# Gate weights for all 128 first keys in one pass over the tokens, beside the second half of the expert activations

## The chip, the cores and the metric

One core of a Trainium2 chip runs the program. The metric is the device time of one execution in microseconds.

## The reference, cut to what matters

Two transformer blocks run one after the other on 256 tokens of width 1024. The change touches the feed-forward part of the first, a layer of 16384 experts with one vector each for input and output. For each token and each of 8 heads it scores 128 first and 128 second keys, takes the best 16 pairs, and sums 16 experts:

```python
cand_i = (top_i[..., 0, :, None] * PEER_KEYS + top_i[..., 1, None, :]).reshape(b, s, PEER_HEADS, PEER_TOPK * PEER_TOPK)
best_v, best_pos = lax.top_k(cand_v, PEER_TOPK)
idx = jnp.take_along_axis(cand_i, best_pos, axis=-1)
gate = jax.nn.softmax(best_v, axis=-1)
...
u = u_tab[ix]
act = jax.nn.gelu(jnp.einsum('chkd,cd->chk', u, hx).astype(jnp.float32))
vv = v_tab[ix]
return jnp.einsum('chk,chkd->cd', (gx * act).astype(vv.dtype), vv)
```

## The kernel before

The kernel doesn't gather experts. It computes all 16384 activations for all tokens, builds a dense matrix of gate weights (zero for experts that a token did not choose), multiplies the two and multiplies the product with the whole value table. An expert is a pair of a first and a second key. A tile holds one first key: 128 second keys on the partitions, tokens along the free dimension. `act[0]` holds first keys 0 to 63, `act[1]` 64 to 127, each 64 x 256 fp32 per partition.

Weights come as fp32 items of 128 x 1024, loaded by SP (`Stream._load`, line 186). ScalarE rounds an item to a high half (line 200), VectorE subtracts to get the low half (line 211), and every product is three fp32r matmuls (line 366): high x high, high x low, low x high. Three pairs of halves exist at a time. When TensorE's next item is taken, `ahead` first issues the low halves still owed, then loads and high halves; with `st.lag` set, as here, an item's low half is issued one item after its high half. So when item j is taken, the low half of item j + 1 goes to VectorE's queue, behind all that the program wrote for VectorE before. Each engine works through its own instructions in the order in which they are written.

The stages around the change:

- `u_phase(0)` computes activations of keys 0 to 63, beside the rest of the routing (`rt`). `u_phase(1)` does keys 64 to 127. A pair of keys is 48 matmuls of 256 columns into one PSUM bank `pa`, and one GELU on ScalarE (line 1253) into `act`.
- `g_phase(half)` builds the gate weights of 64 first keys and multiplies them into `act[half]`. A block is 8 tokens. `prep` makes one-hots in fp16: of the second key (`a`, line 1281), of the first key (`b`, line 1279), and `b` times the gate's high and low part (`c`, line 1283). The 128 partitions of these are the 8 x 16 chosen experts of a token. For each token two matmuls, `a` as weights and the two parts of `c` as moving data, give 128 second keys x 64 first keys (line 1295). VectorE scales that and multiplies it into `act` (line 1297). In `a`, `b` and `c` the 8 tokens are innermost, so the columns of one token lie 8 elements (16 bytes) apart.
- `v_phase(0)` and `v_phase(1)` multiply `act[0]` and `act[1]` with the value table: 12 matmuls of 512 columns for each first key, into four banks `pb` that are summed over both. `need` splits `act` into high and low parts ahead of that.

`weave(main, (side, n))` writes n steps of the side generator after each step of the main one. `g_phase(0)` is woven into `u_phase(1)` at 1.05 steps for each of 64 steps, `g_phase(1)` into `v_phase(0)` at 1.04; each has 64 steps. The one-hot buffers lie in `xt` (the residual, saved to DRAM as `x1d` and loaded back on POOL's queue, line 1348) and in `misc`.

Of the kernel before, what the change touches and what calls it, by code (L numbers as in the profile page):

```python
# [7 lines left out]
F32 = mybir.dt.float32  # L8
FR = mybir.dt.float32r
BF = mybir.dt.bfloat16  # L10
HF = mybir.dt.float16
I32 = mybir.dt.int32
U32 = mybir.dt.uint32
AF = mybir.ActivationFunctionType
OP = mybir.AluOpType
AX = mybir.AxisListType
PSUM = bass.MemoryType.PSUM
# [250 lines left out]
def weave(main, *sides):  # L268

    sides = [[s[0], s[1], s[2] if len(s) > 2 else 0, 0.0] for s in sides]  # L270
    for n, _ in enumerate(main):
        for s in sides:
            if n < s[2]:
                continue
            s[3] += s[1]
            while s[3] >= 1.0 and s[0] is not None:
                s[3] -= 1.0
                if next(s[0], "end") == "end":
                    s[0] = None
# [21 lines left out]
def run(g):  # L301
    for _ in g:
        pass
# [13 lines left out]
def program(ctx, tc, A, out, dbg=None, stop=None, force=False):  # L317
    nc = tc.nc
    V, T, G, E = nc.vector, nc.scalar, nc.gpsimd, nc.tensor

    def dump(name, ap):
        if dbg is not None and name in dbg:
            nc.gpsimd.dma_start(dbg[name], ap)
# [5 lines left out]
    def pool(stack, name, bufs=1, side=None):  # L329
        kw = {} if side is None else {"side": side}  # L330
        return stack.enter_context(tc.tile_pool(name=name, bufs=bufs, reuse_waits="tile", **kw))

    const = pool(ctx, "const")
    strm = pool(ctx, "strm")
    psum = ctx.enter_context(tc.tile_pool(name="psum", bufs=4, space=PSUM))
    resid = pool(ctx, "resid")
    small = pool(ctx, "small", 3)
    x1d = ctx.enter_context(tc.tile_pool(name="dram", bufs=1, space=bass.MemoryType.DRAM)).tile([128, 2, D], F32, name="x1d")
# [11 lines left out]
    def pa():  # L350
        return psum.tile([128, 512], F32, name="pa")

    def pb():
        return psum.tile([128, 512], F32, name="pb")

    def load_const(p, name, eng=None):
        t = p.tile(list(A["c_" + name].shape), F32, name="c_" + name)
        (eng or nc.gpsimd).dma_start(t, A["c_" + name])
        return t
# [5 lines left out]
    def mm(p, a, b, s, e):  # L365
        E.matmul(p, a, b, start=s, stop=e)  # L366
# [23 lines left out]
    def flat(ap):  # L390
        return ap.rearrange("p a b -> p (a b)")
# [84 lines left out]
    xt = resid.tile([128, 2, D], F32, name="xt")  # L476
# [12 lines left out]
    misc = pool(phr, "pmisc", side="right").tile([128, 2048], F32, name="misc")  # L489
# [333 lines left out]
    for m in range(NF):  # L823
        st.add("ffn", A["w_ffn"], 3 * m, 3 * m + 2)
        if m >= LAG:
            q = m - LAG
# [30 lines left out]
    with Pools() as pha:  # L857
# [43 lines left out]
        iota = load_const(const, "iota")  # L901
# [161 lines left out]
        for h in range(6):  # L1063
            heads.append(dict(q=qk[:, h], k=qk[:, 6 + h // 3], v=(lambda kt, h=h: va[:, kt, (h // 3) * 128:(h // 3) * 128 + 128]),
                              base=0, d=128, first=True, last=True, i=h, finish=fin(0), mode="win",
                              scale=128.0 ** -0.5, mask=wmask, sinkb=sinkb))
# [62 lines left out]
    act = [None, pool(ph1, "pR", side="right").tile([128, 64, 256], F32, name="act1")]  # L1129
# [4 lines left out]
    keys = act[1][:, 16:24].rearrange("p a (b c) -> p (a b) c", b=2)  # L1134
# [41 lines left out]
    def routing():  # L1176
        V.tensor_copy(io16, iota[:, :16, None].to_broadcast([128, 16, 16]))
        for tt in range(2):
# [63 lines left out]
    weave(lin_fm("pq", range(0, 16, 2), XH, XL, lambda m, p: T.activation(flat(qf[:, m:m + 2]), p, AF.Copy)),  # L1242
          (rt, 2.7, 8))

    def u_phase(half):
        blk = Blocks("u")
        for k in range(0, 64, 2):
            p = pa()
            for i in range(2):
                fm_tile(p[:, i * 256:i * 256 + 256], blk, 8, XH, XL)  # L1250
                if i == 0:
                    yield
            T.activation(flat(act[half][:, k:k + 2]), p, AF.Gelu_apprx_tanh)  # L1253
            yield

    weave(u_phase(0), (rt, 2.7))
# [1 line left out]
    dump("idT", idT)  # L1258


    io8 = misc[:, 768:1280].bitcast(HF).rearrange("p (a b) -> p a b", b=8)
    ib = misc[:, 1280:1536].bitcast(HF).rearrange("p (a b) -> p a b", a=2)
    gp = misc[:, 1536:1792].bitcast(HF).rearrange("p (a b) -> p a b", a=2)
    V.tensor_copy(io8, iota[:, :, None].to_broadcast([128, 128, 8]))
    V.tensor_copy(ib, idT[:, 0:2])
    V.tensor_scalar(idT[:, 2], idT[:, 2], 32768.0, None, op0=OP.mult)
    V.tensor_copy(gp[:, 0], idT[:, 2])
    V.tensor_sub(gp[:, 1], idT[:, 2], gp[:, 0])

    oha = [xt[:, 0, i * 512:i * 512 + 512].bitcast(HF).rearrange("p (k t) -> p k t", t=8) for i in range(2)]  # L1270
    ohc = [ap.bitcast(HF).rearrange("p (q k t) -> p q k t", q=2, t=8) for ap in (xt[:, 1, 0:512], misc[:, 0:512])]
    ohb = [xt[:, 1, i:i + 256].bitcast(HF).rearrange("p (k t) -> p k t", t=8) for i in (512, 768)]

    def g_phase(half):

        def prep(n):
            t = slice(n * 8, n * 8 + 8)
            a, b, c = oha[n % 2], ohb[n % 2], ohc[n % 2]
            V.tensor_tensor(b, io8[:, half * 64:half * 64 + 64], ib[:, 0, None, t].to_broadcast([128, 64, 8]),
                            op=OP.is_equal)  # L1280
            V.tensor_tensor(a, io8, ib[:, 1, None, t].to_broadcast([128, 128, 8]), op=OP.is_equal)
            for i in range(2):
                V.tensor_tensor(c[:, i], b, gp[:, i, None, t].to_broadcast([128, 64, 8]), op=OP.mult)

        prep(0)
        yield
        for n in range(32):
            if n < 31:
                prep(n + 1)
                yield  # L1290
            a, c = oha[n % 2], ohc[n % 2]
            p = pa()
            for i in range(8):
                for q in range(2):
                    mm(p[:, i * 64:i * 64 + 64], a[:, :, i], c[:, q, :, i], q == 0, q == 1)
            v = act[half][:, :, n * 8:n * 8 + 8]
            V.scalar_tensor_tensor(v, p.rearrange("p (t k) -> p k t", t=8), 2.0 ** -15, v, op0=OP.mult, op1=OP.mult)  # L1297
            yield

    vacc = []  # L1300
# [13 lines left out]
    def v_phase(half, R, after):  # L1314
        need = v_parts(half)

        def part(X):
            def f(k):
                need(k // 2)
                return X[:, k % 8]  # L1320
            return f
        if half == 0:
            vacc.extend([[pb(), pb()] for _ in range(2)])
        for k in range(64 - R):
            need(k // 2)
            h, l = st.take("vt")
            for t in range(2):
                v_mm(half, k, t, h, l)
            yield
        if R:  # L1330
            held = [st.keep("vt") for _ in range(R)]
            for k in range(64 - R, 64):
                need(k // 2)
            yield from halves(held, lambda t, n, i, h, l: v_mm(half, 64 - R + i, t, h, l, (n,)), after)
# [4 lines left out]
            mm_tm(vacc[t][n], h[:, HS[n]], l[:, HS[n]], YH[:, k % 8, ts], YL[:, k % 8, ts],  # L1339
                  half == 0 and k == 0, half == 1 and k == 63)  # L1340

    g0, g1 = g_phase(0), g_phase(1)
    weave(u_phase(1), (g0, 1.05))
    run(g0)
    dump("act0", act[0])
    weave(v_phase(0, 0, None), (g1, 1.04))
    run(g1)
    nc.gpsimd.dma_start(xt, x1d)
    ph0.close()

    st.extend(pool(ctx, "strmc"), 2, 1, len(st.items), "c")
# [55 lines left out]
    pg = pool(phx, "pg", side="right")  # L1407
# [40 lines left out]
    with Pools() as ph:  # L1448
# [40 lines left out]
        for h in range(12):  # L1489
            b = (h % 2) * 64  # L1490
            heads.append(dict(q=qs[b:b + 64, h // 2], k=kap(h // 4, b),
                              v=(lambda kt, h=h: vs[:, kt, (h // 4) * 64:(h // 4) * 64 + 64]), base=b, d=64,
# [17 lines left out]
    with Pools() as ph:  # L1510
# [10 lines left out]
        for m in range(NF):  # L1521
            p = pa()
# [20 lines left out]
    with Pools() as ph:  # L1543
# [70 lines left out]
        for h in range(12):  # L1614
            b = (h % 2) * 64
            heads.append(dict(q=qf[b:b + 64, h // 2], k=qf[b:b + 64, 6 + h // 2],
                              v=(lambda kt, h=h: vf[:, kt, h * 64:h * 64 + 64]), base=b, d=64,
# [121 lines left out]
    with Pools() as ph:  # L1739
# [186 lines left out]
        for n in range(NE * 11):  # L1926
            e, j = divmod(n, 11)
# [23 lines left out]
        e, yp = NE - 1, yps.pop(NE - 1)  # L1951
        gBe, bBe = st.spare(), st.spare()
        ln_load(3, gBe, bBe)
        a = turn(last)
# [6 lines left out]
        b = [small.tile([128, 2, 6], F32, name="bn") for _ in range(2)]  # L1961
# [34 lines left out]
```

## Time and profile before

| | us |
|---|---|
| median of 3 runs | 2499.32 |
| lowest run | 2498.3 |
| profiled execution | 2496.38 |
| its span, first to last instruction | 2494.6 |

The profile is one execution, taken by the hardware profiler. Engines are PE (TensorE's matmuls), PEld (its weight loads, which overlap matmuls), DVE (VectorE), ACT (ScalarE), POOL and SP. Times are microseconds unless marked ns; `out<-in` are the program's tile names, L366 is line 366. The ends of matmuls are modelled, so the step from one start to the next tells more than the length. Idle time of an engine that isn't the bound costs nothing.

### The profile page before, as it was taken

How to read it: one execution, taken by the hardware profiler on the slowest of the kernel's cores; microseconds unless marked ns; L12 is line 12 of the kernel's file. 1: busy time of each engine (PE TensorE's matmuls, PEld its weight loads, DVE VectorE, ACT ScalarE, POOL GpSimd, SP SyncE). 2: the span in 40 equal slices, each digit the busy share in tenths (PEclk: the TensorE clock that was granted, in tenths of full speed). 3: DMA queues.
4: the chain of work that ended last, by engine and by line, in shares of the span. 5: the costliest groups of instructions: out<-in, count | busy, mean ns of one | idle time of the engine just before them, and what ended most of it. 6: DMA issues, size and time to landing. Idle time of an engine off the chain costs nothing. (4 is left out here: it accounts for less than half of the span.)

```text
span 2494.6 us, 38669 instructions
## 1 busy us (share of the span) xinstructions
PE 2439.9 (98%) x14776; PEld 2125.6 (85%) x14776; DVE 1880.2 (75%) x2923; ACT 1393.0 (56%) x1859; POOL 35.2 (1%) x48
## 2 busy tenths in 40 slices
PE   9999999999999999999999999989899999999997
PEld 8888999999999888788868998768788888888885
DVE  7776669886666666665677548579889999999997
ACT  5775444443333333454544444438677877877775
POOL 0100000000000000000000000000000000000000
PEclk9999999999999999999999999989999999999999
DMA  7345555554444444756524554359899999999992
GB/s 266 117 132 181 186 178 180 175 173 133 143 136 141 139 135 143 254 187 190 174 93 178 186 195 146 121 217 336 307 340 346 368 341 344 366 355 338 363 357 89
DMA packets 149652, 545.62 MB, mean 219 GB/s; under 512 B 16960, under 2 KB 17088, under 8 KB 148816
## 3 DMA queue, kind: packets, MB, share of 16 engines
q1 hardware_dynamic: 145728, 528.55, 61.5%
q0 software_dynamic: 2720, 10.50, 1.3%
q10 hardware_dynamic: 1008, 4.00, 0.4%
q8 instruction: 118, 1.93, 0.3%
q14 instruction: 78, 0.64, 0.1%
HBM read 540.88 MB, written 2.10 MB: 218 GB/s over the span
## 5 line engine op out<-in xcount | busy, mean ns | idle before, releaser
L200 ACT ACTIVATE hwb<-rawb 128x1024 fp32r<-128x1024 f32 (+1 forms) x406 | 428.5, 1057 | 333.6 <-PE pa L366 132.5
L211 DVE TENSOR_TENSOR lwb<-rawb,hwb 128x1024 fp32r<-128x1024 f32 (+1 forms) x406 | 493.5, 1224 | 77.0 <-ACT hwb L200 75.1
L366 PE MATMUL pa<-XH,hwb 128*128 128x256 f32 x1848 | 509.1, 283 | 0.4 <-ACT XH L502 0.3
L366 PE MATMUL pa<-XH,lwb 128*128 128x256 f32 x1848 | 501.8, 280 | 2.7 <-DVE lwb L211 2.6
L366 PE MATMUL pa<-XL,hwb 128*128 128x256 f32 x1848 | 500.9, 279 | 0.0
L366 PEld LDWEIGHTS pa<-XH,hwb 128*128 128x128 f32 x1848 | 341.6, 188 | 4.4 <-issue 1.3
L366 PEld LDWEIGHTS pa<-XH,lwb 128*128 128x128 f32 x1848 | 340.2, 188 | 5.1 <-DVE lwb L211 4.9
L366 PEld LDWEIGHTS pa<-XL,hwb 128*128 128x128 f32 x1848 | 340.5, 188 | 1.1
L211 DVE TENSOR_TENSOR lwb<-rawe,hwb 128x1024 fp32r<-128x1024 f32 x176 | 210.9, 1222 | 23.9 <-ACT hwb L200 19.0
L200 ACT ACTIVATE hwb<-rawe 128x1024 fp32r<-128x1024 f32 x176 | 185.7, 1058 | 25.5 <-PE pb L366 11.6
L211 DVE TENSOR_TENSOR lwb<-rawf,hwb 128x1024 fp32r<-128x1024 f32 x130 | 156.6, 1222 | 17.8 <-ACT hwb L200 13.0
L1297 DVE SCALAR_TENSOR_TENSOR act<-pa,act 128x512 f32<-128x512 f32 x64 | 44.3, 692 | 164.2 <-PE pa L366 164.2
L366 PE MATMUL pb<-hwb,XH 128*128 128x512 f32 (+1 forms) x428 | 166.5, 389 | 1.2 <-ACT XH L387 1.2
L366 PE MATMUL pb<-hwb,XL 128*128 128x512 f32 (+1 forms) x428 | 165.5, 387 | 0.0
L366 PE MATMUL pb<-lwb,XH 128*128 128x512 f32 (+1 forms) x428 | 164.9, 385 | 0.0
L366 PE MATMUL pa<-hwb,XH 128*128 128x512 f32 x396 | 159.0, 401 | 0.0
L366 PE MATMUL pa<-hwb,XL 128*128 128x512 f32 x396 | 156.8, 396 | 0.0
L366 PE MATMUL pa<-lwb,XH 128*128 128x512 f32 x396 | 156.2, 395 | 0.0
L200 ACT ACTIVATE hwb<-rawf 128x1024 fp32r<-128x1024 f32 x130 | 137.1, 1059 | 23.2 <-PE pa L366 11.4
L366 PEld LDWEIGHTS <-xt 128*128 128x128 f16 x1024 | 119.9, 147 | 10.3 <-issue 8.9
L1253 ACT ACTIVATE act<-pa 128x512 f32<-128x512 f32 x64 | 38.3, 599 | 156.1 <-PE pa L366 156.1
L366 PE MATMUL pb<-hwb,aH 128*128 128x512 f32 x264 | 104.5, 396 | 0.0
(606 smaller groups left out, 5172.0 us busy)
## 6 DMA issues: line engine op xcount, KB each, us to landing
rawe<-w_e SPq DMA_DIRECT2D x220, 512.0 KB, 5.2
rawf<-w_e SPq DMA_DIRECT2D x152, 512.0 KB, 5.2
rawb<-w_u SPq DMA_DIRECT2D x128, 512.0 KB, 3.6
rawb<-w_e SPq DMA_DIRECT2D x112, 512.0 KB, 5.3
rawb<-w_vt SPq DMA_DIRECT2D x110, 512.0 KB, 3.6
rawb<-w_ffn SPq DMA_DIRECT2D x47, 512.0 KB, 4.4
rawc<-w_e SPq DMA_DIRECT2D x44, 512.0 KB, 5.1
rawb<-w_mrg SPq DMA_DIRECT2D x36, 512.0 KB, 3.7
```

Of the source, the lines that this page charges most:

```text
L200: self.nc.scalar.activation(h[:, :n], r[:, :n], AF.Copy)
L211: self.nc.vector.tensor_sub(l[:, :n], r[:, :n], h[:, :n].bitcast(F32))
L366: E.matmul(p, a, b, start=s, stop=e)
L1253: T.activation(flat(act[half][:, k:k + 2]), p, AF.Gelu_apprx_tanh)
L1297: V.scalar_tensor_tensor(v, p.rearrange("p (t k) -> p k t", t=8), 2.0 ** -15, v, op0=OP.mult, op1=OP.mult)
```

## The change

- `g_phase` no longer takes a half: 32 blocks of 8 tokens, each for all 128 first keys, so matmuls of 128 columns into a tile `pg` of two PSUM banks. All of it is woven into `u_phase(1)`, at 1.56 steps for each of its 64; the generator has 96 steps (two for each `prep`, one for the matmuls and what reads them). `v_phase(0)` runs alone.
- One-hots are laid out as 4 pairs of tokens x 128 keys x 2 tokens, so the columns of one token lie 2 elements (4 bytes) apart. All four instructions of a `prep` have 1024 elements. The source that carries the tokens' keys or gates is read with the pair of tokens innermost, the same pair 128 times over.
- When a block comes, only some activations exist. `seen` counts the keys and tokens written so far. For keys that have their activation, VectorE multiplies the gates into `act` as before (keys 0 to 63 always, then those of the second half so far). For the other keys ScalarE copies the scaled gates into `act`. `u_phase` in turn computes GELU in two pieces: for tokens whose gates are already there it writes GELU back into PSUM and VectorE multiplies it into `act`; for the others it writes `act` as before.
- PSUM: the `pb` banks get a pool of their own, closed for the two `pg` tiles and opened again before `v_phase(0)`.
- `misc` is laid out anew, the table of keys `io2` repeats each key 2 times instead of 8, and the load of `xt` is issued before `v_phase(0)`.

```diff
--- before.py
+++ after.py
@@ -333,6 +333,15 @@
     const = pool(ctx, "const")
     strm = pool(ctx, "strm")
     psum = ctx.enter_context(tc.tile_pool(name="psum", bufs=4, space=PSUM))
+    bank_b = Pools()
+    ctx.push(lambda *e: bank_b.close())
+
+    def psum_b(n, name):
+
+        bank_b.close()
+        return bank_b.enter_context(tc.tile_pool(name=name, bufs=n, space=PSUM))
+
+    psb = [psum_b(4, "psb")]
     resid = pool(ctx, "resid")
     small = pool(ctx, "small", 3)
     x1d = ctx.enter_context(tc.tile_pool(name="dram", bufs=1, space=bass.MemoryType.DRAM)).tile([128, 2, D], F32, name="x1d")
@@ -351,7 +360,7 @@
         return psum.tile([128, 512], F32, name="pa")
 
     def pb():
-        return psum.tile([128, 512], F32, name="pb")
+        return psb[0].tile([128, 512], F32, name="pb")
 
     def load_const(p, name, eng=None):
         t = p.tile(list(A["c_" + name].shape), F32, name="c_" + name)
@@ -1242,6 +1251,10 @@
     weave(lin_fm("pq", range(0, 16, 2), XH, XL, lambda m, p: T.activation(flat(qf[:, m:m + 2]), p, AF.Copy)),
           (rt, 2.7, 8))
 
+
+
+    seen = {"k": 0, "t": 0}
+
     def u_phase(half):
         blk = Blocks("u")
         for k in range(0, 64, 2):
@@ -1250,7 +1263,15 @@
                 fm_tile(p[:, i * 256:i * 256 + 256], blk, 8, XH, XL)
                 if i == 0:
                     yield
-            T.activation(flat(act[half][:, k:k + 2]), p, AF.Gelu_apprx_tanh)
+            n, pv, to = seen["t"], p.rearrange("p (k t) -> p k t", k=2), act[half][:, k:k + 2]
+            if n == 0:
+                T.activation(to, pv, AF.Gelu_apprx_tanh)
+            else:
+                T.activation(pv[:, :, :n], pv[:, :, :n], AF.Gelu_apprx_tanh)
+                if n < 256:
+                    T.activation(to[:, :, n:], pv[:, :, n:], AF.Gelu_apprx_tanh)
+                V.tensor_mul(to[:, :, :n], pv[:, :, :n], to[:, :, :n])
+            seen["k"] += 2
             yield
 
     weave(u_phase(0), (rt, 2.7))
@@ -1258,43 +1279,55 @@
     dump("idT", idT)
 
 
-    io8 = misc[:, 768:1280].bitcast(HF).rearrange("p (a b) -> p a b", b=8)
-    ib = misc[:, 1280:1536].bitcast(HF).rearrange("p (a b) -> p a b", a=2)
-    gp = misc[:, 1536:1792].bitcast(HF).rearrange("p (a b) -> p a b", a=2)
-    V.tensor_copy(io8, iota[:, :, None].to_broadcast([128, 128, 8]))
+    io2 = misc[:, 1024:1152].bitcast(HF).rearrange("p (a b) -> p a b", b=2)
+    ib = misc[:, 1536:1792].bitcast(HF).rearrange("p (a b) -> p a b", a=2)
+    gp = misc[:, 1792:2048].bitcast(HF).rearrange("p (a b) -> p a b", a=2)
+    V.tensor_copy(io2, iota[:, :, None].to_broadcast([128, 128, 2]))
     V.tensor_copy(ib, idT[:, 0:2])
     V.tensor_scalar(idT[:, 2], idT[:, 2], 32768.0, None, op0=OP.mult)
     V.tensor_copy(gp[:, 0], idT[:, 2])
     V.tensor_sub(gp[:, 1], idT[:, 2], gp[:, 0])
 
-    oha = [xt[:, 0, i * 512:i * 512 + 512].bitcast(HF).rearrange("p (k t) -> p k t", t=8) for i in range(2)]
-    ohc = [ap.bitcast(HF).rearrange("p (q k t) -> p q k t", q=2, t=8) for ap in (xt[:, 1, 0:512], misc[:, 0:512])]
-    ohb = [xt[:, 1, i:i + 256].bitcast(HF).rearrange("p (k t) -> p k t", t=8) for i in (512, 768)]
-
-    def g_phase(half):
+    oha = [xt[:, 0, i * 512:i * 512 + 512].bitcast(HF).rearrange("p (u k j) -> p u k j", u=4, j=2) for i in range(2)]
+    ohc = [ap.bitcast(HF).rearrange("p (q u k j) -> p q u k j", q=2, u=4, j=2) for ap in (xt[:, 1], misc[:, 0:1024])]
+
+    def g_phase(ps):
 
         def prep(n):
-            t = slice(n * 8, n * 8 + 8)
-            a, b, c = oha[n % 2], ohb[n % 2], ohc[n % 2]
-            V.tensor_tensor(b, io8[:, half * 64:half * 64 + 64], ib[:, 0, None, t].to_broadcast([128, 64, 8]),
-                            op=OP.is_equal)
-            V.tensor_tensor(a, io8, ib[:, 1, None, t].to_broadcast([128, 128, 8]), op=OP.is_equal)
-            for i in range(2):
-                V.tensor_tensor(c[:, i], b, gp[:, i, None, t].to_broadcast([128, 64, 8]), op=OP.mult)
-
-        prep(0)
-        yield
+            a, c = oha[n % 2], ohc[n % 2]
+
+            def pairs(x, i):
+                return x[:, i, n * 8:n * 8 + 8].rearrange("p (u j) -> p u j", j=2)[:, :, None].to_broadcast([128, 4, 128, 2])
+
+            keys = io2[:, None].to_broadcast([128, 4, 128, 2])
+            V.tensor_tensor(c[:, 0], keys, pairs(ib, 0), op=OP.is_equal)
+            V.tensor_tensor(a, keys, pairs(ib, 1), op=OP.is_equal)
+            yield
+            for i in (1, 0):
+                V.tensor_tensor(c[:, i], c[:, 0], pairs(gp, i), op=OP.mult)
+            yield
+
+        yield from prep(0)
         for n in range(32):
             if n < 31:
-                prep(n + 1)
-                yield
+                yield from prep(n + 1)
             a, c = oha[n % 2], ohc[n % 2]
-            p = pa()
+            p = ps.tile([128, 1024], F32, name="pg")
             for i in range(8):
+                u, j = i // 2, i % 2
                 for q in range(2):
-                    mm(p[:, i * 64:i * 64 + 64], a[:, :, i], c[:, q, :, i], q == 0, q == 1)
-            v = act[half][:, :, n * 8:n * 8 + 8]
-            V.scalar_tensor_tensor(v, p.rearrange("p (t k) -> p k t", t=8), 2.0 ** -15, v, op0=OP.mult, op1=OP.mult)
+                    mm(p[:, i * 128:i * 128 + 128], a[:, u, :, j], c[:, q, u, :, j], q == 0, q == 1)
+            pv = p.rearrange("p (t k) -> p k t", t=8)
+            ts, K = slice(n * 8, n * 8 + 8), seen["k"]
+            for half in range(2):
+                lo, hi = half * 64, half * 64 + 64
+                m = min(max(K, lo), hi)
+                if m > lo:
+                    v = act[half][:, :m - lo, ts]
+                    V.scalar_tensor_tensor(v, pv[:, lo:m], 2.0 ** -15, v, op0=OP.mult, op1=OP.mult)
+                if m < hi:
+                    T.activation(act[half][:, m - lo:, ts], pv[:, m:hi], AF.Copy, scale=2.0 ** -15)
+            seen["t"] += 8
             yield
 
     vacc = []
@@ -1339,13 +1372,13 @@
             mm_tm(vacc[t][n], h[:, HS[n]], l[:, HS[n]], YH[:, k % 8, ts], YL[:, k % 8, ts],
                   half == 0 and k == 0, half == 1 and k == 63)
 
-    g0, g1 = g_phase(0), g_phase(1)
-    weave(u_phase(1), (g0, 1.05))
-    run(g0)
+    g = g_phase(psum_b(2, "psg"))
+    weave(u_phase(1), (g, 1.56))
+    run(g)
+    psb[0] = psum_b(4, "psb2")
     dump("act0", act[0])
-    weave(v_phase(0, 0, None), (g1, 1.04))
-    run(g1)
     nc.gpsimd.dma_start(xt, x1d)
+    run(v_phase(0, 0, None))
     ph0.close()
 
     st.extend(pool(ctx, "strmc"), 2, 1, len(st.items), "c")
```

## Rows read from the trace of the kernel before

**Rows 1.** Profile page: busy time by engine; lines of the chain that ended last.

```profile
PE 2439.9 (98%) x14776; PEld 2125.6 (85%) x14776; DVE 1880.2 (75%) x2923; ACT 1393.0 (56%) x1859; POOL 35.2 (1%) x48
...
PE pa L366 18%; PE pb L366 9%; PE pa L1902 1%; DVE xt L577 0%; DVE bn L1969 0%; DVE xt L579 0%; PE pa L1771 0%; DVE yL L1807 0%; ACT yH L1806 0%; DVEq L1992 0%; DVE rs L523 0%; ACT aH L387 0%; DVE rs L532 0%; DVE mv L575 0%; DVE rs L533 0%
```

**Rows 2.** Windows (us, busy and instructions by engine, clock, DMA): activations, values 1, 2.

```profile
546.00:787.00 241.00, 240.48 (x2028) 238.74 (x2026) 145.97 (x224) 82.29 (x95) 0.00 (x0) 1.00 0.45 140
788.00:1029.00 241.00, 241.00 (x1278) 202.07 (x1279) 165.84 (x257) 84.98 (x98) 4.21 (x8) 1.00 0.45 140
1040.00:1180.00 140.00, 138.58 (x598) 112.56 (x597) 84.96 (x94) 73.60 (x87) 0.00 (x0) 1.00 0.66 213
```

**Rows 3.** Waits (us, times, longest) of the activation stage, then of the value stage.

```profile
DVE act L1297 <- PE pa L366: 90.5, 32, 3.1
...
PEld pa L366 <- DVE lwb L211: 0.5, 1, 0.5
PE pa L366 <- DVE lwb L211: 0.3, 1, 0.3
...
POOL xt L1348 <- PE pa L366: 722.5, 1, 722.5
```

**Rows 4.** Timeline, activation stage (start, length in us; idle before), around one gate block.

```profile
640.57 0.28 PE L366 MATMUL pa<-XH,lwb 128*128 128x256 f32 x1
...
640.68 2.14 PE L366 MATMUL pa<-xt 128*128 128x64 f16 x16
640.88 0.60 ACT L1253 ACTIVATE act<-pa 128x512 f32<-128x512 f32 x1 [1.88 <-PE pa L366]
...
642.78 0.28 PE L366 MATMUL pa<-XL,hwb 128*128 128x256 f32 x1
...
642.86 0.69 DVE L1297 SCALAR_TENSOR_TENSOR act<-pa,act 128x512 f32<-128x512 f32 x1 [3.07 <-PE pa L366]
...
643.47 1.22 DVE L211 TENSOR_TENSOR lwb<-rawb,hwb 128x1024 fp32r<-128x1024 f32 x1
...
644.61 0.42 DVE L1279 TENSOR_TENSOR xt<-misc 128x512 f16<-128x512 f16 x1
...
644.94 0.69 DVE L1281 TENSOR_TENSOR xt<-misc 128x1024 f16<-128x1024 f16 x1
...
645.54 0.76 DVE L1283 TENSOR_TENSOR xt<-xt,misc 128x512 f16<-128x512 f16 x2
```

**Rows 5.** Timeline, first value stage, around one gate block.

```profile
951.73 0.40 PE L366 MATMUL pb<-lwb,XH 128*128 128x512 f32 x1
...
951.96 0.40 PE L366 MATMUL pb<-hwb,XL 128*128 128x512 f32 x1
...
954.42 0.40 PE L366 MATMUL pb<-lwb,XH 128*128 128x512 f32 x1
```

**Rows 6.** Groups by line, activation stage: xcount | busy us, mean ns | idle before, releaser.

```profile
L200 ACT ACTIVATE hwb<-rawb 128x1024 fp32r<-128x1024 f32 x63 | 66.8, 1060 | 60.1 <-PE pa L366 60.1
L366 PEld LDWEIGHTS <-xt 128*128 128x128 f16 x512 | 60.0, 147 | 1.3
...
L1253 ACT ACTIVATE act<-pa 128x512 f32<-128x512 f32 x32 | 19.2, 600 | 99.4 <-PE pa L366 99.4
```

**Rows 7.** Groups by line, 290 to 310 us: bf16 matmuls and loads.

```profile
L366 PE MATMUL pa<-c_ident 128*128 128x256 bf16 x24 | 2.8, 272 | 0.0
...
L366 PEld LDWEIGHTS <-c_ident 128*128 128x128 bf16 x24 | 2.4, 98 | 0.3
```

**Rows 8.** Timeline, first matmul of the first value stage.

```profile
787.95 0.50 PE L366 MATMUL pb<-hwb,XH 128*128 128x512 f32 x1 [1.20 <-ACT XH L387]
```

**Rows 9.** Groups by line, routing stage, 370 to 545 us: instructions with repeated sources.

```profile
L1229 DVE TENSOR_REDUCE act<-act 128x64 f32<-128x1024 bf16 x8 | 18.2, 2270 | 0.1
...
L1226 DVE TENSOR_TENSOR act<-act 128x1024 bf16<-128x1024 bf16 x8 | 9.8, 1221 | 0.1
...
L1198 DVE TENSOR_TENSOR act<-act 128x256 f32<-128x256 f32 x16 | 6.0, 414 | 0.0
```

## The prediction

> **What bounds the kernel now.** I read the page first: TensorE is busy 98% of the span and the chain that ended last runs on its matmuls, while VectorE is at 75% and ScalarE at 56% [rows 1]. So a microsecond taken from TensorE's stream is worth a microsecond as long as the other engines still feed it. Next the windows, because the change lives in two stages only: the second half of the activations (546 to 787 us) and the first half of the value products (788 to 1029 us). In both TensorE is busy all the time at a granted clock of 1.00, VectorE 61% and 69%, and the DMA share is 0.45 [rows 2]. The waits say the same from the other side: in the first stage VectorE's product waits 90.5 us in all for TensorE, and TensorE 0.8 us for VectorE's low halves of the weights [rows 3]. Both stages are therefore TensorE streams, and what the change is worth is what it takes out of them, less what new VectorE work puts back.
>
> **What a gate block costs now.** One block covers 8 tokens and 64 first keys: 16 half-precision weight loads and 16 matmuls of 64 columns. In the value stage the matmul before it starts at 951.96, and the second one behind it at 954.42; at the 0.23 pitch of its neighbours that one would have started at 952.42, so the block costs 2.00 us [rows 5]. In the activation stage the step of the other matmuls is 0.117 (241 us less 32 x 2.00, over 2028 - 512 of them [rows 2]), and the block costs 640.57 to 642.78 less two steps, 1.98 us [rows 4]. There are 64 blocks, 32 in either stage (the 512 loads of one stage are 32 x 16 [rows 6]).
>
> **Part 1: the blocks leave the value stage.** After the change 32 blocks with 128 columns each do all first keys, all beside the second activations. The first value stage loses 32 x 2.00 = 64 us. A second view agrees: it now does 1278 matmuls in 241 us, 512 of them the blocks'; the second value stage, which has no blocks, does 598 in 140 us, so the remaining 766 need 179 us, 62 less, with loads that keep up at a DMA share of 0.66 [rows 2]. The reload of the residual moves ahead of this stage. It is one 1 MB transfer on POOL's queue, where now it waits 722.5 us for the last block's matmuls [rows 3] because the one-hots lie in its target; nothing else of POOL's stands behind it until the second value stage, and SP's loads share the DMA engines with it at a share of 0.66. It is wanted only behind the second value stage, so it costs nothing.
>
> **Part 2: the price of a block of 128 columns.** The trace has no such block. From below: matmuls of 256 bf16 columns follow each other at (2.8 - 0.27)/23 = 0.11 us [rows 7], so 128 columns cost 0.055 and a block 16 x 0.055 = 0.88 us. From above: nothing gets faster and it stays 2.00. In the trace each load takes as long as the step to the next matmul, and 64 columns are too few to explain 0.12 us, so I take the load as the limit. A half-precision load, whose elements lie 16 bytes apart, takes 147 ns; a bf16 load of the same shape from adjacent elements 98 ns [rows 6, 7]. With token pairs innermost the step is 4 bytes, which is nearer to the latter: 16 x 0.049 = 0.78 us less, 1.22 us a block. That is 32 x 0.78 = 25 us more off TensorE.
>
> [...]
>
> **Part 3: what VectorE and ScalarE get.** Their time per pair of activation tiles (TensorE 48 x 0.117 = 5.62, with a block 6.84) is worked out in steps from start to start [rows 4]. Two low halves, 1.14 each (643.47 to 644.61): 2.28, as before. Four one-hot instructions of 1024 elements instead of one such and three of 512: 0.60 each (644.94 to 645.54), 2.40. One scaled product of 512, 0.61; it reads PSUM 128 columns apart and over two banks instead of 64 apart in one, which I take as free, since its 0.69 now is in line with the 1.22 of a low half, which reads 1024 adjacent elements. New are a second product and a multiply behind the activation, both growing from 0 to 512 elements over the stage: 0.08 to 0.61, mean 0.35 each. Sum 2.28 + 2.40 + 0.61 + 0.70 = 5.99 of 6.84, at the end 6.5. So VectorE isn't the bound by its sum. ScalarE gets one more piece of the activation and a shrinking copy, under 1 us a pair against over 60% idle [rows 2].
>
> By order it can be. VectorE works its queue in order, and the new multiply stands ahead of the low half that TensorE needs next but one. Take time 0 as the moment TensorE leaves a pair. The activation starts 0.20 later (640.68 to 640.88). In two pieces it lasts 0.60 and one fixed part of some 0.14 (600 ns for 512 elements, 1060 for the 1024 of a weight's high half [rows 6]), so the multiply starts at about 1.0 and ends at 1.35 in mid-stage. Behind it come the gate steps that the weave puts there (A and B: two one-hots each, 1.20; M: the matmuls and products), then the low half, 1.22. TensorE wants it after one tile of 24 matmuls (2.81) and two more (0.23), and after the block if that comes first. With M and A behind the pair: the products wait for the block (1.22 + 0.20 = 1.42), end at 2.38, A at 3.58, the low half at 4.80; wanted at 1.22 + 2.81 + 0.23 = 4.26. TensorE stalls 0.5. With A alone behind it: 1.35 + 1.20 + 1.22 = 3.77, no stall. Going through the 1.56 steps a tile, what stands behind the pair | in its middle: M A | B, 3 early pairs at 0.3 and 5 late at 0.75; A | B M, 4 at 0 and one at 0.25; A B | M, 4 at 0.6; B | M A, 4 at 0.45; B M | A, 5 at 0.5; M | A B, 3 at 0.15. Sum 12 us. From below it is 0, if the low halves come early enough, as now (under 1 us, [rows 3]). From above: the first piece of the activation is written back to PSUM, which nothing in the trace does on ScalarE; at twice its 0.60 every multiply is 0.6 late, and the stalls about double, 24 us. I take 12, since the rows give every other duration.
>
> **What is free.** The change of stage costs the same wait as now (TensorE idles 1.20 us until ScalarE has split the first activations, [rows 8]), plus the last multiply, 0.6. The new PSUM pools replace one that nothing has used since the merge, and the last block is out of them before the value sums want the banks. The smaller key table lies on VectorE beside TensorE's work.
>
> **Sum.** Against the profiled execution, 2496.4 us (span 2494.6): 64 + 25 - 12 - 0.6 = 76 less, 2420. The median of the runs shown is 2.9 above that execution, so 2423.
>
> **Rivals.**
> *The load isn't the limit.* If a block stays at 2.00, the stalls shrink to 7 (TensorE comes later): 64 - 7 - 0.6 = 56, 2443. For it: every matmul starts with the next load, so either could be the limit. Against: the 147 and 98 ns.
>
> *No stalls, cheapest block.* 0.88 a block and nothing late: 64 + 32 x 1.12 = 100, 2399. For it: VectorE's sum fits. Against: the order above, which tightens as TensorE gets faster.
>
> *One-hots at one element a cycle.* Each now compares against a pair of tokens that is read over and over; the trace shows 0.69 us for runs of 8 tokens [rows 4], and 1.22 where a source repeats a single 16-bit element [rows 9]. At that price A and B last 2.28 each. With A B behind the pair the low half is ready at 1.35 + 4.56 + 1.22 = 7.1 against 4.26, 9.7 us a pair; over all patterns the same working gives 8.5 to 9.7, mean 9.0, instead of 5.62 + 2.00 = 7.62 now: 1.38 x 32 = 44 lost, 20 gained, 2479. Against: a source that repeats one 32-bit word 16 times costs 414 ns for 256 elements [rows 9], no more than the 0.69 for 512 and 1.22 for 1024 of 32 bits lead to (0.69 - 0.53/2 = 0.42 [rows 4]). [...]
>
> *Slower than before.* The same place, a worse price: the dearest 1024-element instruction of 16 bits in the trace takes 2270 ns [rows 9]. Four of those, at 2.19 from start to start, bring VectorE alone to 2.28 + 8.76 + 0.61 + 0.70 = 12.35 us a pair, and (12.35 - 7.62) x 32 - 64 = 87 is lost: 2586. It decides where a pair takes 7.62 + 2.00 = 9.62, at about 1.4 us an instruction (9.0 at 1.22, and four times 0.16 more); only a read that breaks the stream at each pair would do that, and no repeated source in [rows 9] shows it (the 2270 ns are a strided sum).
>
> **How the numbers follow.** Forecast 0.55, load not the limit 0.15, no stalls 0.14, one element a cycle 0.10, slower 0.06. The first three hold 0.84 and reach from 2399 to 2443; with the bounds of the stalls (0 to twice 12) 2398 to 2458 holds 8 in 10. 2%, about what a measurement of this kernel can tell from no change, is 50 us: below 2449. Faster: 0.55 + 0.14 + 0.11 of the 0.15 = 0.80; within 2%: 0.04 + 0.10 = 0.14; slower 0.06.
>
> **What would show it.** In the profile after: no half-precision loads in the first value stage, which spans about 178 us; 512 loads in all, near 98 ns, blocks of about 1.2 us; one-hots of 0.69 us; waits of TensorE for the low halves of some 12 us in the activation stage, 7.2 us a pair. Loads still at 147 ns, or one-hots over 1 us, would make the second or third step wrong, and waits beyond 40 us the sum.

## The result and the profile after

The kernel after takes 2421.4 us (median of 4 runs, 2420.3 to 2422.6); the kernel before, run beside it, 2498.8. One of the four runs of the kernel before took 4474.0 us, and the ratio leaves it out. The ratio is 0.969, with a 95% interval of 0.9675 to 0.9709: 3.1% faster. The time is 2 us from the forecast. Two of the terms behind it were each off by 7 to 9 us, in opposite directions, and the reason given for one of them is wrong.

First the page of the kernel after: span and busy time by engine.

```profile
span 2420.8 us, 37592 instructions
PE 2352.5 (97%) x14264; PEld 2040.6 (84%) x14264; DVE 1862.3 (77%) x2825; ACT 1406.0 (58%) x1920; POOL 35.2 (1%) x48
```

TensorE has 512 matmuls less than before [rows 1] and is still the engine that sets the time. Its busy time fell by 87 us and the span by 74: some 13 us of waiting are new. The windows tell where (columns as in [rows 2]; the rows are the activation stage and the first value stage without their edges):

```profile
546.00:779.00 233.00, 218.25 (x2040) 211.20 (x2039) 196.78 (x290) 96.47 (x158) 0.53 (x1) 1.00 0.44 147
780.00:957.00 177.00, 176.94 (x766) 144.80 (x766) 97.67 (x98) 84.42 (x97) 4.75 (x9) 1.00 0.59 196
```

The value stage is a pure TensorE stream of 766 matmuls, against 1278 in 241 us [rows 2]. In the activation stage TensorE idles 14.75 of 233 us, against 0.52 of 241 before, and VectorE is busy 84% of the time instead of 61%. The waits of that stage name the cause (engine, what it waited for, us in all, times, longest):

```profile
ACT act L1329 <- DVE act L1327: 82.6, 29, 4.7
ACT pa L1270 <- PE pa L375: 36.6, 23, 3.1
DVE act L1273 <- ACT act L1272: 28.8, 28, 1.8
PEld pa L375 <- DVE lwb L211: 19.4, 27, 1.3
PE pa L375 <- DVE lwb L211: 13.3, 20, 1.1
```

TensorE's weight loads wait 27 times for a low half of VectorE's (19.4 us; once and 0.5 us before, [rows 3]). VectorE waits 28 times for the second piece of the activation (L1272) before its multiply (L1273); what is queued behind it is late by as much. The new instructions of the stage, by line and form (xcount | busy us, mean ns of one | idle before):

```profile
L375 PEld LDWEIGHTS <-xt 128*128 128x128 f16 x512 | 29.5, 97 | 1.3
L1307 DVE TENSOR_TENSOR misc<-misc 128x1024 f16<-128x1024 f16 x32 | 22.0, 688 | 0.6
L1304 DVE TENSOR_TENSOR xt<-misc 128x1024 f16<-128x1024 f16 x32 | 21.9, 685 | 0.0
L1327 DVE SCALAR_TENSOR_TENSOR act<-pg,act 128x512 f32<-128x512 f32 x32 | 21.9, 685 | 3.9 <-PE pg L375 3.9
L1270 ACT ACTIVATE pa<-pa 128x496 f32<-128x496 f32 x1 | 0.6, 576 | 0.0
```

The loads take 97 ns instead of 147 [rows 6]. Each one-hot takes 685 to 688 ns, as L1281 did for 8 tokens innermost [rows 4]. The scaled product over two PSUM banks costs 685 ns, what it cost in one (0.69 us, [rows 4]). ScalarE's write back into PSUM takes 576 ns for 496 elements, in line with the 600 for 512 into SBUF [rows 6].

The stages can be measured from first matmul to first matmul (the second value stage to its last). In the table "block" is what one block adds to TensorE's stream (activation stage; the matmul steps around it subtracted, as in the prediction), "stalls" the sum of what other steps of that stage exceed 0.117 us by (steps over 0.147 us alone). That is more than the 13.3 us of waits above, which count only the time behind a matmul's modelled end. Stages and blocks come from the profiled execution of each kernel, the medians from the timed runs.

| kernel | median | activation stage | first values | second values | block | stalls |
|---|---|---|---|---|---|---|
| before | 2498.8 | 244.7 | 241.6 | 180.9 | 1.98 | 0.6 |
| after | 2421.4 | 234.6 | 177.9 | 178.9 | 0.99 | 21.3 |
| layout alone, 64 columns | 2413.2 | 201.1 | 197.7 | 183.4 | 0.58 | 0.7 |
| weights at 16 bytes | 2423.8 | 236.1 | 178.0 | 178.9 | 1.13 | 18.4 |
| moving data at 16 bytes | 2514.8 | 326.8 | 178.0 | 178.9 | 3.69 | 26.7 |
| both at 16 bytes (merge alone) | 2515.7 | 326.3 | 178.0 | 178.9 | 3.80 | 23.6 |
| both at 8 bytes | 2439.2 | 250.3 | 178.0 | 178.9 | 1.90 | 9.4 |
| low halves first | 2403.9 | 217.4 | 178.0 | 178.9 | 0.99 | 3.6 |
| low halves at each tile | 2422.1 | 230.4 | 181.6 | 178.9 | 1.05 | 14.9 |
| late reload | 2423.3 | 234.5 | 177.9 | 179.7 | 0.99 | 21.3 |

(In the two rows with slow moving data "stalls" also holds steps at half clock, a granted 0.50, see the last section.) From before to after the span falls by 73.8: activation stage 10.1, first values 63.7, second values 2.0, less 1.5 and 0.5 in what comes ahead and behind. The stage begins between 543.1 and 544.8 us in all the profiles, without order, so the 1.5 are scatter.

### The profile page after: what moved, and what is told of

Its sections match the earlier page's. It is cut to its first block, busy times and chain, and to the rows that moved or that the text cites. A ratio compares the mean times of both kernels' runs of the same rounds, so it can differ in the third digit from the quotient of the medians.

```text
span 2420.8 us, 37592 instructions
## 1 busy us (share of the span) xinstructions
PE 2352.5 (97%) x14264; PEld 2040.6 (84%) x14264; DVE 1862.3 (77%) x2825; ACT 1406.0 (58%) x1920; POOL 35.2 (1%) x48
## 5 line engine op out<-in xcount | busy, mean ns | idle before, releaser
L211 DVE TENSOR_TENSOR lwb<-rawe,hwb 128x1024 fp32r<-128x1024 f32 x176 | 210.9, 1222 | 24.0 <-ACT hwb L200 19.4
L211 DVE TENSOR_TENSOR lwb<-rawf,hwb 128x1024 fp32r<-128x1024 f32 x130 | 156.6, 1222 | 17.8 <-ACT hwb L200 13.7
L397 DVE TENSOR_TENSOR XL<-act,XH 128x512 fp32r<-128x512 f32 x64 | 44.1, 691 | 109.3 <-ACT XH L396 109.3
L375 PE MATMUL pb<-lwb,aH 128*128 128x512 f32 x264 | 104.0, 394 | 0.0
L375 PE MATMUL pb<-hwb,aL 128*128 128x512 f32 x264 | 104.0, 394 | 0.0
```

What stands on the lines that cost most here:

```text
L211: self.nc.vector.tensor_sub(l[:, :n], r[:, :n], h[:, :n].bitcast(F32))
L397: V.tensor_sub(l, src, h.bitcast(F32))
```

## Experiments

### The layout alone

The change does two things: it lays tokens out in pairs, and it merges the two passes over the tokens into one. This kernel is the one before with the first alone: two passes, 64 columns, blocks beside both stages.

```diff
...
-    oha = [xt[:, 0, i * 512:i * 512 + 512].bitcast(HF).rearrange("p (k t) -> p k t", t=8) for i in range(2)]
+    oha = [xt[:, 0, i * 512:i * 512 + 512].bitcast(HF).rearrange("p (u k j) -> p u k j", u=4, j=2) for i in range(2)]
...
-                    mm(p[:, i * 64:i * 64 + 64], a[:, :, i], c[:, q, :, i], q == 0, q == 1)
+                    mm(p[:, i * 64:i * 64 + 64], a[:, i // 2, :, i % 2], c[:, q, i // 2, :, i % 2], q == 0, q == 1)
```

> The kernel before with the new layout alone: token pairs innermost in all one-hots, still 64 blocks of 64 columns, half of them in the value stage. Theory (the weight load with its 16-byte step was the limit): loads fall from 147 to 97 ns as in the changed kernel; if the load still sets the step, 64 columns cost the 0.0585 us of the changed kernel's 128, a block 0.99 instead of 2.0 us, 64 x 1.0 = 64 us less than before, 2435. Rival (in the changed kernel the 128 columns set the step): the step falls further, to about 0.035, a block to 0.6, 64 x 1.4 = 88 less, 2411. If the layout is worth nothing and the wider blocks gave all: no change, 2499.

Measured: 2413.2 us, ratio 0.965 (0.9636 to 0.9668). It is faster than the kernel after. Its loads and matmuls over the whole run, as groups by form:

```profile
L366 PEld LDWEIGHTS <-xt 128*128 128x128 f16 x1024 | 34.4, 98 | 10.3 <-issue 8.9
L366 PE MATMUL pa<-misc,xt 128*128 128x64 f16 x512 | 21.1, 193 | 0.0
```

The matmul takes 193 ns where it took 302 with 8 tokens innermost, and the next one starts 0.030 us later instead of 0.122: a load "lasts" 98 ns, but does not hold up the matmuls. A block costs 0.58 us instead of 1.98. So the layout explains the whole gain; the merge on top of it costs 8 us. TensorE's block time does fall, by 32 x (0.58 + 0.60 - 0.99) = 6 us (0.60 is the block in this kernel's value stage), but the stalls take 21. Over the two stages that hold blocks in one kernel or the other the merge costs 13.7 us (412.5 against 398.8 in the table); 4.5 come back in the second value stage, which has no blocks and is longer in this kernel (183.4 against 178.9, see the reload below).

### Which operand's step costs: weights or moving data

The prediction took the weight load as what paces a block. Three kernels tell the operands apart: the kernel after with the old 8-token order for the weights `a` alone, for the moving `c` alone, and for both. The last is the merge without the layout. All have 128 columns.

```diff
# weights at 16 bytes
...
-                    mm(p[:, i * 128:i * 128 + 128], a[:, u, :, j], c[:, q, u, :, j], q == 0, q == 1)
+                    mm(p[:, i * 128:i * 128 + 128], a[:, :, i], c[:, q, u, :, j], q == 0, q == 1)
# moving data at 16 bytes
...
-                    mm(p[:, i * 128:i * 128 + 128], a[:, u, :, j], c[:, q, u, :, j], q == 0, q == 1)
+                    mm(p[:, i * 128:i * 128 + 128], a[:, u, :, j], c[:, q, :, i], q == 0, q == 1)
```

> The changed kernel with only the weights' one-hot (second keys) in the old order, 8 tokens innermost; the moving operand keeps token pairs. Theory (the load's 16-byte step was the limit): loads of 147 ns, a step of 0.12 us, a block 2.0 instead of 0.99: 32 us more on TensorE, of which its present stalls of 21 us absorb about half, 2437 to 2453. Rival (the moving operand's step was the limit): a step of 0.0585 as in the changed kernel, 2421.

> The changed kernel with only the moving one-hots (first keys times gates) in the old order, 8 tokens innermost; the weights keep token pairs. Theory (the load's step was the limit): loads of 97 ns, a step near 0.0585, 2421. Rival (the moving read was the limit, 64 columns at 16 bytes in 0.12 us): 128 columns take 0.24, a block 3.9 us, 93 us more on TensorE less the stalls it absorbs, about 2500.

> The changed kernel with both one-hots in the old order, 8 tokens innermost: the merge into one pass without the new layout. If the moving operand's 16-byte step sets the pace (as the run with that alone in the old order showed, 3.69 us a block), the load's step hides behind it: 2510 to 2520. If load and moving operand add up: 0.229 + 0.006 us a matmul, 3.8 us a block, 2518.

Measured: weights at 16 bytes 2423.8 us (0.9685 to 0.9717 of before); moving data 2514.8 (1.0048 to 1.0081); both 2515.7 (1.0056 to 1.009). Groups by form, first of the kernel with the weights at 16 bytes:

```profile
L375 PEld LDWEIGHTS <-xt 128*128 128x128 f16 x512 | 35.2, 147 | 1.4
L375 PE MATMUL pg<-misc,xt 128*128 128x128 f16 x256 | 19.9, 231 | 0.0
```

and of the kernel with the moving data at 16 bytes:

```profile
L375 PE MATMUL pg<-misc,xt 128*128 128x128 f16 x256 | 61.0, 406 | 0.0
L375 PEld LDWEIGHTS <-xt 128*128 128x128 f16 x512 | 56.7, 116 | 50.6
```

The load is back at 147 ns in the first, and the step from matmul to matmul is only 0.064 us instead of 0.058: it overlaps, and a block costs 1.13 - 0.99 = 0.14 us more. In the second the step is 0.229, four times as long, and the loads idle 50.6 us before them. So the moving operand sets the pace: at 16 bytes a step takes 0.229 us, at 4 bytes 0.058 to 0.064 with either layout of the weights. (The total of this kernel is 15 us above the "about 2500" expected for that case: the stalls were not absorbed but came to 26.7, most of them steps at half clock, see the last section.)

The four corners: neither part 2499, layout 2413, merge 2516, both 2421. The merge alone loses 17 us: its blocks at 32 x 3.80 us cost as much as both sets before (122 against 64 x 1.98 = 127), and the stage's 23.6 us under "stalls" come on top, of which 17.0 are steps at half clock (last section).

### A step between: 8 bytes

This kernel keeps the merge and puts 4 tokens innermost, so that the columns of one token lie 8 bytes apart.

```diff
...
-    oha = [xt[:, 0, i * 512:i * 512 + 512].bitcast(HF).rearrange("p (u k j) -> p u k j", u=4, j=2) for i in range(2)]
+    oha = [xt[:, 0, i * 512:i * 512 + 512].bitcast(HF).rearrange("p (u k j) -> p u k j", u=2, j=4) for i in range(2)]
...
-                u, j = i // 2, i % 2
+                u, j = i // 4, i % 4
```

> The changed kernel with four tokens innermost, so both operands have a step of 8 bytes, two elements in 16 bytes. If each new 16-byte line costs the moving read a fixed time (0.229 us for 128 columns at 16 bytes, one line each): half, 0.115 us a matmul, a block 1.85, 27 us more on TensorE of which stalls absorb some 10: 2432 to 2445. If two elements in a line are enough for the full rate: a step of 0.058, 2421.

Measured: 2439.2 us (0.9746 to 0.9778). Groups by form:

```profile
L375 PEld LDWEIGHTS <-xt 128*128 128x128 f16 x512 | 56.0, 118 | 1.9
L375 PE MATMUL pg<-misc,xt 128*128 128x128 f16 x256 | 32.9, 297 | 0.0
```

The steps, with the count of 16-byte stretches that one matmul's columns touch:

| moving step | columns | 16-byte stretches | step us | per stretch ns |
|---|---|---|---|---|
| 16 bytes (before) | 64 | 64 | 0.122 | 1.9 |
| 16 bytes (moving data alone) | 128 | 128 | 0.229 | 1.8 |
| 8 bytes | 128 | 64 | 0.118 | 1.8 |
| 4 bytes (after) | 128 | 32 | 0.058 | 1.8 |
| 4 bytes (layout alone) | 64 | 16 | 0.030 | 1.9 |

One price of 1.8 to 1.9 ns per stretch fits all five. At 4 bytes the columns would need as much by themselves: 256 adjacent bf16 columns step at 0.11 us [rows 7], an estimate of 0.055 for 128. By that estimate a step below 4 bytes would gain next to nothing (0.003 us a matmul); no run has one. Two elements in a stretch do not do as well as four: 0.118 us against 0.058, so the second case of the expectation, 2421, is out. Whether the price is for a stretch of 16 bytes or for the distance as such (0.11 to 0.12 ns for each byte that the columns span fits the five as well), no run here tells.

### The low half ahead of the multiply

The stalls were put down to order: VectorE's multiply waits for ScalarE, and the low half that TensorE needs next stands behind it. This kernel is the one after with one line, which issues the low half that is owed before the multiply instead of behind it. No work is added.

```diff
                 if n < 256:
                     T.activation(to[:, :, n:], pv[:, :, n:], AF.Gelu_apprx_tanh)
+                st.lows()
                 V.tensor_mul(to[:, :, :n], pv[:, :, :n], to[:, :, :n])
```

> The changed kernel with the owed low half of the weights issued on VectorE ahead of the multiply behind the activation, instead of behind it and the gate steps; the work is the same. Theory (order: the multiply waits for the activation and holds up the low half): TensorE's 21 us of stalls in the activation stage fall to about 3, which remain where matmuls and products stand in the middle of a pair: 2403. Rival (VectorE's sum of 6.0 us a pair and its fixed costs are the limit): the stalls only move to the other low half, 2421.

Measured: 2403.9 us, ratio 0.962 (0.9604 to 0.9636), faster than both kernels and than the layout alone. Windows, then groups by form, of its activation stage:

```profile
546.00:762.00 216.00, 213.29 (x2040) 210.33 (x2038) 198.94 (x291) 96.99 (x159) 0.53 (x1) 1.00 0.49 160
```

```profile
L375 PE MATMUL pa<-XH,lwb 128*128 128x256 f32 x512 | 143.9, 281 | 1.6 <-DVE lwb L211 1.4
...
L1274 DVE TENSOR_TENSOR act<-pa,act 128x496 f32<-128x496 f32 x1 | 0.7, 668 | 0.0
```

VectorE does the same work (198.9 us) in 216 us instead of 233, 92% busy. TensorE's idle time for low halves falls from 13.3 to 1.4 us, the stalls by the steps from 21.3 to 3.6. The low half that changed its place is that of a pair's second tile: second tiles hold 17.1 of the 21.3 us and 1.3 of the 3.6, first tiles 4.2 and 2.3. The multiply hardly waits any more (1.3 us for the second piece of the activation instead of 28.8): when VectorE comes to it, that piece is mostly done. So the stalls were order, not VectorE's sum. With them gone this kernel is 9 us faster than the layout alone, but the table gives the merge itself only 3.4 of these (395.4 against 398.8 over the activation and first value stages); 4.5 are the second value stage's, and the rest is within the scatter of the runs.

### Low halves earlier yet

```diff
                 fm_tile(p[:, i * 256:i * 256 + 256], blk, 8, XH, XL)
+                st.lows()
                 if i == 0:
                     yield
```

> The changed kernel with the owed low half issued behind every tile's matmuls, so ahead of the gate steps in the middle of a pair too. Theory (order): the 3.6 us of stalls left with the low half issued once a pair go as well, 2400. Rival: here the high half that it needs is not yet there (ScalarE makes it when TensorE has left the tile before, and works on the activation first), VectorE waits about 1 us a pair in front of its queue, and at 6.0 us of work in a pair of 6.6 that comes back as stalls: 2404 to 2412.

Measured: 2422.1 us (0.968 to 0.9712), no better than the kernel after and dearer than either expectation. The waits of its activation stage:

```profile
ACT act L1330 <- DVE act L1328: 120.3, 31, 5.1
DVE lwb L211 <- ACT hwb L200: 30.3, 27, 1.6
PEld pa L375 <- DVE lwb L211: 13.4, 19, 1.1
PE pa L375 <- DVE lwb L211: 9.5, 15, 0.9
```

Issued straight behind each tile, the low half stands at VectorE's head before ScalarE has made its high half: 27 waits, 30.3 us, in which the gate work behind it stands still, and the stalls are back at 14.9. At 680 us, for one, that high half stands in ScalarE's queue behind the copy of the gates (L1330), which has waited 4.7 us for VectorE's product (L1328): each queue holds up the other. The activation stage loses 13.0 us against the low halves first, and the first value stage 3.6 more (181.6 against 178.0), most of it at half clock (last section: a mean clock of 0.68 over 10 us, by estimate 0.32 x 10 = 3.2 us). The place matters both ways.

### The reload late again

The second value stage became 2.0 us shorter, which nothing in the forecast asked for. In the kernel with the layout alone, where the reload of `xt` still waits for the last block of the value stage, it takes 183.4 (some 1.5 us of it are steps at half clock behind a gap, last section). This kernel is the one after with the reload issued behind the load of `gB`, which POOL can issue only at the end of the first value stage.

```diff
-    nc.gpsimd.dma_start(xt, x1d)
     run(v_phase(0, 0, None))
...
     nc.gpsimd.dma_start(gB0, rows(A["gfin"], D))
+    nc.gpsimd.dma_start(xt, x1d)
```

> The kernel after, with one line moved: the reload of xt (1 MB on POOL's queue) is issued behind the load of gB, which POOL can only issue at the end of the first value stage (in the kernel after gB waits 173.7 us for the last split of the first activations). So the reload again falls together with gB, the tables and the 1 MB load of misc, as in the kernel before. Theory A, the reload's place is what made the second value stage 2.0 us shorter (180.89 us before, 178.92 after; 183.42 with the layout alone, where the reload is late too): the second value stage takes 180.9 to 183.4 us again, with a gap of TensorE some 11 us into it that waits for a high half whose raw item landed late, and the other stages stay within 0.5 us; the total 2423 to 2426 us. Theory B, the 2.0 us have another cause: the stage stays at 178.9 us and the total at 2421 us. The total can hardly tell 2 us; the length of the stage in the trace can, which is 178.92 us in all kernels with the early reload.

Measured: 2423.3 us (0.968 to 0.9712), which the medians cannot tell from the kernel after; the trace can. The second value stage takes 179.7 us, 0.8 more, and the other two what they did. The timeline of TensorE in this kernel, 10.9 us into the stage (start, length; idle before and releaser):

```profile
967.17 0.40 PE L375 MATMUL pb<-lwd,XH 128*128 128x512 f32 x1
967.40 0.40 PE L375 MATMUL pb<-hwd,XL 128*128 128x512 f32 x1
968.06 0.50 PE L375 MATMUL pb<-hwd,XH 128*128 128x512 f32 x1 [0.26 <-ACT XH L396]
```

ScalarE waits 3.3 us there for a raw item, and the split of the activations stands behind that wait. In the kernel before the same step, also 10.9 us into the stage, is 1.82 us instead of 0.23; with the early reload it is not there. How the loads shared the DMA engines over the first 14 us of the stage (the row of POOL's queue in the DMA view: packets, MB, share of the 16 engines' time), in the kernel before, with the late reload, and after:

```profile
q0 software_dynamic: 524, 1.89, 37.1%
```

```profile
q0 software_dynamic: 296, 1.36, 24.4%
```

```profile
q0 software_dynamic: 64, 0.39, 6.8%
```

The engines are busy nine tenths or more of nearly the whole stretch in all three (mean share 0.98 or more), so what POOL's queue takes is taken from the weight items, whose queue has 60.5%, 75.4% and 95.2%: 37%, 24% and 7% of POOL's go with stages of 180.9, 179.7 and 178.9 us. With the late reload it is not the reload itself that falls into the stage: the 1 MB load of `misc` waits 4.3 us for it in POOL's queue and is issued at 955.58, 0.9 us ahead of the stage, instead of 951.46 (5.8 ahead) in the kernel after. That only 0.8 of the 2.0 came back fits the place, too: here the reload starts 10.3 us ahead of the stage (946.2), in the kernel before 4.9 (1024.7). So the reload's place is shown as a cause; that it is the whole of the 2.0 us is argued from these shares.

## Why the prediction was right, and where it was not

- **The blocks leave the value stage: right.** Forecast 64, measured 63.7; 177.9 us against "about 178", with the 766 matmuls counted out of [rows 2], and no half-precision load in it.
- **The price of a block of 128 columns: the sign right, the reason wrong, the size off.** Forecast 1.22, measured 0.99, so 32 x 0.99 = 31.7 us saved instead of 25. The failed step is "I take the load as the limit". It read a load of 147 ns as "as long as" a step of 0.122 us, but the two differ: the loads overlap, 512 of 147 ns (75 us) in 60.0 us of busy time [rows 6]. And weights and moving data had the same 16-byte step, so no row of before told which of them sets the pace. The runs show the moving operand instead: at 16 bytes alone it makes the step 0.229 us, the weights alone 0.064. The bound from below, 0.88, stood: it came from rows of 256 adjacent columns at 0.11 us [rows 7]. The first rival, that the load isn't the limit, was right in its name and wrong in its price (2.00 a block, 2443): it took an unchanged limit for granted, when the change brought the moving columns closer together too.
- **One-hots at the old price: right.** 683 to 688 ns against 0.69. The rivals that price a repeated pair of tokens higher (1.22 us an instruction, and the slower one at about 1.4) fell with it: the same pair of 16-bit elements, read 128 times over, costs here what runs of 8 tokens cost before.
- **Stalls: the mechanism right, the size low.** Forecast 12 with bounds 0 and 24, measured 21.3. The kernel with low halves first shows that the order makes them. Part of the miss follows from the block: the shorter it is, the earlier TensorE wants its half (stalls 9.4 at 1.90 us a block, 18.4 at 1.13, 21.3 at 0.99). By the forecast's own two points (7 at 2.00, 12 at 1.22) 0.99 would have given 13.5. The working followed only the low half of the second tile; the 4.2 us in first tiles have no term in it. Nor has the step behind a stall, which is 0.10 us too long in 28 places, some 3 us in all, part of them in first tiles. What made the rest is not shown. The upper bound's reason, a doubled ScalarE write to PSUM, is not it: that write costs what its neighbours cost (576 ns for 496 elements into PSUM, 583 for as many into `act`).
- **The last multiply: forecast 0.6, not found.** TensorE idles 1.20 us ahead of the first value matmul, as before [rows 8]. The activation stage is 10.1 us shorter: 31.7 of blocks, less 20.7 of stalls, less 0.9 spread over steps too little above 0.117 to count as stalls.
- **The reload "costs nothing": it gains.** The step looked at what its new place collides with, and not at what its old place had cost: up to 2 us in the second value stage, of which 0.8 were reproduced.
- **The sum.** The block's miss (7 us too dear) and the stalls' (9 too cheap) nearly cancel. The time was right; a reader who took the reasons with it would have looked for the rest of the gain in the weight loads, whose step is worth 2 us (2423.8 against 2421.4), instead of VectorE's queue, where 17 lay.

## What to carry to other kernels

Look at the step in bytes of a matmul's moving operand, not only at its columns: packing what one matmul reads closer together was worth more here (85 us alone) than halving the number of the blocks' matmuls (17 us lost alone). When two durations in a trace are close, ask whether they share a cause before one is named the limit of the other; a kernel that changes one operand alone settles it. And where work moves onto an engine that works its queue in order, as VectorE did here (28.8 us of waits ahead of the low halves), place each waiting instruction behind what the critical engine needs next: one line moved was worth 17 us, and the same line behind every tile, too early, gave it back.

## What the hardware showed that was not expected

The granted clock of TensorE fell while it had work all the time. In the kernel with both operands at 16 bytes, a block of 16 matmuls runs from 704.01 us to 707.58 at a step of 0.23. Windows of that kernel: the activation stage; most of the block; right behind it; later.

```profile
546.00:869.00 323.00, 318.43 (x2027) 273.59 (x2025) 197.52 (x286) 97.43 (x157) 0.54 (x1) 0.92 0.33 108
704.00:707.00 3.00, 3.00 (x15) 1.96 (x14) 0.52 (x1) 0.00 (x0) 0.00 (x0) 0.97 0.50 157
707.60:710.20 2.60, 2.60 (x14) 2.60 (x13) 2.22 (x5) 1.11 (x2) 0.00 (x0) 0.50 0.03 8
710.30:714.00 3.70, 3.70 (x23) 2.85 (x23) 2.31 (x4) 0.88 (x3) 0.00 (x0) 1.00 0.42 130
```

Behind the block the clock is 0.50, and the steps of 256 columns are 0.21 us instead of 0.117, with TensorE busy 2.60 of 2.60 us; 2.7 us behind the block it is back at 1.00. TensorE did nothing before it but the block's slow matmuls, after a stream at full clock that idled 0.37 us once, near 701. The whole stage has 0.92 (0.91 with the moving data alone at 16 bytes). In the kernels with blocks of 2 us or less the stage shows 1.00 (before, after, layout alone, weights at 16 bytes, both at 8 bytes, low halves first and at each tile). So here fast matmuls were slow, too, behind a block of slow ones; that the block is the cause fits the order in time and the 1.00 of the other kernels, and no run shows it alone. The steps that lie in the stretches at 0.50 account for 17.0 of the 23.6 us that the table has under "stalls" for this kernel, and for 21.8 of 26.7 with the moving data alone at 16 bytes. So less than 7 us of either are waits; whether TensorE would have waited longer at full clock is not shown.

The clock also fell in two other kernels, there behind idle time. First the second value stage of the layout alone, where TensorE had idled 2.38 us; then the first value stage with low halves at each tile, where it had idled 1.82 and 0.89 us.

```profile
957.00:962.00 5.00, 5.00 (x15) 3.64 (x15) 5.00 (x6) 3.51 (x5) 0.00 (x0) 0.66 1.01 406
```

```profile
775.00:785.00 10.00, 9.82 (x30) 7.84 (x31) 4.18 (x6) 2.64 (x3) 0.00 (x0) 0.68 0.49 147
```

In both stretches steps of 512 columns reach 0.43 us instead of 0.23, so part of what these two stages lose is the clock's.
